# Sample tokens kept in residue order modulo 16 through the attention of an encoder layer

## The chip, the cores and the metric

The kernel runs on one core of one Trainium2 chip. The metric is device microseconds of one execution; lower is better. TensorE is called PE, VectorE DVE, ScalarE ACT, GpSimd POOL and SyncE SP in the rows. PEld is the loading of PE's stationary operand, which overlaps its matmuls.

## The reference

One encoder layer is applied to a prompt of 256 tokens and to a sample sequence of 2048 tokens, width 1024. A mixing sublayer projects the normed input into u, q, k and v; u goes through a state-space branch, q, k and v through attention of 8 heads of 64, and both are normed, joined and projected. A feed-forward sublayer with a short convolution follows. All operands are float32. The attention is what the change is about:

```python
DILATED_PATTERNS = ((128, 1), (512, 4), (2048, 16))

def dilated_attention(q, k, v):
    slopes = jnp.exp2(-8.0 * jnp.arange(1, N_HEADS + 1, dtype=jnp.float32) / N_HEADS)
    outs, lses = [], []
    for window, dil in DILATED_PATTERNS:
        o, lse = dilated_branch(q, k, v, window, dil, slopes)
        outs.append(o)
        lses.append(lse)
    weights = jax.nn.softmax(jnp.stack(lses, axis=0), axis=0)
    return jnp.sum(weights[..., None] * jnp.stack(outs, axis=0), axis=0)
```

In `dilated_branch`, a pattern of dilation d splits the tokens into d subsequences by their residue modulo d. In each of them a query sees the keys at most 64 places away on either side, with a bias that falls linearly with the distance in tokens and with the slope of the head. The three results are mixed per token by the softmax of their log denominators.

## The kernel before

The program is built in Python with all loops unrolled. A scheduler places the instructions in each engine's queue by a simulated timeline of its own; each engine then runs its queue strictly in order, with semaphores between engines. DMAs are issued from SP's queue, the loads of q and k (L939) and a few others from POOL's.

Stages, in order of time. The first norms the tokens and projects u and v, 256 tokens at a time. The second projects q and k while the state-space branch runs; `qk_d` holds q and k transposed, split into a high and a low part, and `v_d` holds v, all in token order. The third is the attention, from about 680 to 1165 us. The fourth projects the attention's half of the mixture, norms again, and the last two are the feed-forward's up and down projections.

The attention runs over four head pairs `hp`, two heads `h` each. `load_values` fetches the values of a head pair in three layouts, `v1`, `v2`, `v3`, one for each dilation 1, 4 and 16, and `vq` for the prompt. `load_head` fetches `qs` (queries, high part above low part), `kh` and `kl` of one head, 2304 tokens each. A head makes its three patterns in order 0, 1, 2 (dilations 1, 4, 16), then the mixing weights of the patterns, then the prompt's attention, then the join.

A pattern has 16 units of 128 queries. A unit of dilation 1 or 4 scores them against 256 keys, one of dilation 16 against its 128. At the ends of a subsequence there are only 192 keys. The operands are taken from `qs`, `kh` and `kl` by slices with a step of 1, 4 or 16 elements (`span`); queries are the stationary operand, keys the moving one. Units are worked in groups of 512 score columns (`group`): two matmuls for each unit (L967 with `kh`, L968 with `kl`), VectorE adds the bias and finds the row's extreme (L973), ScalarE takes the exponential and its sum (L974), PE transposes the probabilities (L153), and `copy2` evicts them (L957 on ScalarE, L958 on VectorE). `pair` multiplies them with the values (L1004), two units at a time in the two halves of PE's columns; for dilation 16 L1125 does this. An end block has 64 keys where others have 128. ScalarE evicts the outputs to `ot`, back into token order (L1128, L1130, L1133).

GpSimd makes the head's bias tables `bt` from constants (L1073 to L1077). The extreme and the sum of each query (`st`) go through DRAM for patterns 0 and 1 (L1143 writes those of pattern 1), since `weights` wants them with 16 consecutive tokens in a partition (`r01`, L1010); pattern 2 has them so already. `weights` writes the mixing weights to `w_d`; `join` loads them broadcast over partitions (`wb`, L1036), and GpSimd multiplies and adds the three outputs (L1041, L1043) and stores them in `ob_d`.

Between groups, `side_work` lets another piece of work run: in the first head pair the gated unit of the state-space branch (`glu`), later the projection of that branch's output (`project_a`, tile names `pat`, `pah`, `ppa`, `pxt`). Those matmuls are 512 columns wide and stand in PE's queue between those of the attention; `pah` is made by ScalarE and GpSimd (L868). What is left of them is done after the last head, before `project_b` works on the joined outputs, prompt tiles first.

## Time and profile before

| | us |
|---|---|
| three runs | 2893.41 median, 2881.18 to 2896.9 |
| the profiled execution, its own time | 2889.24 |
| its span from first to last instruction | 2887.4 |
| PE busy in the span | 2760.7 |
| VectorE busy | 1864.3 |
| ScalarE busy | 1325.5 |
| GpSimd busy | 649.3 |

The mean granted clock of TensorE over the span is 0.974 of full speed. A slice below is a fortieth of the span, 72 us. [...]

### The profile page before, as it was taken

To read this page: it belongs to the slowest core of one execution; us is meant where nothing else is said; L and a number is where in the kernel's file an instruction comes from. 1 tells how busy PE (TensorE), PEld (TensorE's weight loads), DVE (VectorE), ACT (ScalarE), POOL (GpSimd) and SP (SyncE) were. 2 spreads that over 40 slices of the span, in tenths; PEclk is the share of its full clock that TensorE was granted. 3 is DMA by queue.
4 is the path that set the end of the run, shared out by engine and by line. 5 is a ranking of instruction groups with operands and counts; after the bars stand their busy time and mean duration, and the time that the engine had idled before them with its cause. 6 is when DMAs were issued, how large, how long until landed. Compare 5 with 4: busy or idle time off the path is not lost. (4 is left out here: it accounts for less than half of the span.)

```text
span 2887.4 us, 43596 instructions
## 1 busy us (share of the span) xinstructions
PE 2760.7 (96%) x15488; PEld 2458.3 (85%) x15488; DVE 1864.3 (65%) x4274; ACT 1325.5 (46%) x2723; POOL 649.3 (22%) x1120
## 2 busy tenths in 40 slices
PE   7998989999999999889999999999999989999999
PEld 6787767788778888667999999999999978888887
DVE  5766899976645444597989897778877752223221
ACT  3354455545566666344655565556555531112110
POOL 0587533312243442220111121113100000000000
PEclk9999999999899999999999999999999999999999
DMA  7574888777676775747555564444544452224221
GB/s 214 160 245 138 249 232 233 197 189 166 138 188 159 165 179 134 231 157 255 180 172 179 174 199 155 156 154 138 161 154 152 134 186 83 74 86 141 84 86 47
DMA packets 483990, 471.04 MB, mean 163 GB/s; under 512 B 87984, under 2 KB 406076, under 8 KB 480700
## 3 DMA queue, kind: packets, MB, share of 16 engines
q1 hardware_dynamic: 465084, 425.25, 49.3%
q0 software_dynamic: 18688, 43.01, 6.5%
q8 instruction: 122, 2.00, 0.3%
q14 instruction: 96, 0.79, 0.1%
HBM read 308.63 MB, written 159.55 MB: 162 GB/s over the span
## 5 line engine op out<-in xcount | busy, mean ns | idle before, releaser
L156 PE MATMUL pf<-dw,ah 128*128 128x512 f32 x792 | 309.7, 392 | 4.3 <-ACT dw L1182 4.3
L157 PE MATMUL pf<-dw,ah 128*128 128x512 f32 x792 | 309.4, 391 | 2.0 <-DVE dw L1183 2.0
L158 PE MATMUL pf<-dw,ah 128*128 128x512 f32 x792 | 309.1, 391 | 0.0
L1467 DVE TENSOR_TENSOR acc<-pf,acc 128x512 f32<-128x512 f32 x72 | 49.7, 691 | 379.8 <-PE pf L158 379.7
L1453 ACT ACTIVATE ah<-at 128x512 fp32r<-128x512 f32 x72 | 53.1, 784 | 409.0 <-PE pf L158 409.0
L974 ACT ACTIVATE sb<-sb,st 128x256 f32<-128x256 f32 (+2 forms) x384 | 172.5, 452 | 31.6 <-DVE st L973 30.2
L1182 ACT ACTIVATE uw<-su 128x1024 fp32r<-128x1024 f32 x132 | 139.7, 1058 | 100.4 <-PE pu_5p L1366 5.6
L156 PEld LDWEIGHTS pf<-dw,ah 128*128 128x128 f32 x792 | 149.7, 189 | 37.5 <-ACT dw L1182 6.2
L157 PEld LDWEIGHTS pf<-dw,ah 128*128 128x128 f32 x792 | 149.6, 189 | 33.8 <-DVE dw L1183 3.1
L158 PEld LDWEIGHTS pf<-dw,ah 128*128 128x128 f32 x792 | 149.6, 189 | 31.1
L1183 DVE TENSOR_TENSOR uw<-su,uw 128x1024 fp32r<-128x1024 f32 x132 | 160.8, 1219 | 17.8 <-ACT uw L1182 17.5
L1415 ACT ACTIVATE h<-r,convp 128x767 f32<-128x767 f32 (+2 forms) x132 | 135.5, 1028 | 67.0 <-DVE r L1402 64.3
L1410 POOL COPY r<-edge 128x2 f32<-128x2 f32 x88 | 58.2, 662 | 480.3 <-DVE h L1421 471.5
L1418 DVE SCALAR_TENSOR_TENSOR h<-r,convp,h 128x255 f32<-128x255 f32 (+3 forms) x176 | 139.8, 815 | 39.4 <-ACT h L1415 38.9
L1412 POOL COPY edge<-r 128x2 f32<-128x2 f32 x88 | 73.9, 840 | 357.5 <-DVE r L1402 186.0
L967 PE MATMUL s<-kh,qs 128*128 128x256 f32 (+2 forms) x384 | 151.7, 403 | 0.0
L958 DVE COPY pb<-pt 64x128 f32<-64x128 f32 (+2 forms) x150 | 74.2, 505 | 106.6 <-PE pt L153 92.3
L1421 DVE SCALAR_TENSOR_TENSOR h<-r,convp,h 128x768 f32<-128x768 f32 (+2 forms) x176 | 140.6, 813 | 1.4
L968 PE MATMUL s<-kl,qs 128*128 128x256 f32 (+2 forms) x384 | 137.1, 368 | 0.0
L973 DVE CUSTOM_DVE_ANT_0 sb<-s,bt 128x256 f32<-128x256 f32 (+2 forms) x384 | 120.5, 356 | 18.0 <-PE pt L153 13.2
L500 POOL TENSOR_TENSOR q<-ph,phs 128x64 f32<-128x64 f32 (+6 forms) x352 | 119.5, 372 | 2.1
L1004 PE MATMUL po<-pb,v 128*64 128x128 f32 (+1 forms) x1024 | 115.0, 296 | 0.0
(934 smaller groups left out, 7650.7 us busy)
## 6 DMA issues: line engine op xcount, KB each, us to landing
us<-in_w_up_dram SPq DMA_DIRECT2D x88, 512.0 KB
su<-ws_d SPq DMA_DIRECT2D x88, 512.0 KB
at<-act_d SPq DMA_DIRECT2D x36, 704.0 KB
ws_d<-su SPq DMA_DIRECT2D x44, 512.0 KB
qk_d<-qt SPq DMA_DIRECT2D x72, 256.0 KB
wb<-w_d SPq DMA_DIRECT2D x32, 384.0 KB
us<-in_w_up_dram SPq DMA_DIRECT2D x44, 256.0 KB
ds<-in_w_down_dram SPq DMA_DIRECT2D x44, 256.0 KB
```

What stands on the lines that cost most here:

```text
L156: mm = T.matmul(ps, lhi, rhi, start=first, stop=False)
L157: T.matmul(ps, lhi, rlo, start=False, stop=False)
L158: T.matmul(ps, llo, rhi, start=False, stop=last)
L967: T.matmul(ps[:, c:c + n], qs[:, q], khi[:, keys], start=True, stop=False)
L968: T.matmul(ps[:, c:c + n], qs[:, q], klo[:, keys], start=False, stop=True)
L973: V.tensor_tensor_reduce(sb[:, c:c + n], ps[:, c:c + n], bias, 1.0, 3e38, ALU.add, ALU.min, mn)
L974: A.activation(sb[:, c:c + n], sb[:, c:c + n], AF.Exp, bias=mn, scale=-1.0, accum_out=den)
L1182: A.activation(dst[:, 0], src, AF.Copy)
L1183: V.tensor_tensor(dst[:, 1], src, dst[:, 0].bitcast(F32), ALU.subtract)
L1415: A.activation(h[:, a:b], r[:, a:b], AF.Identity, bias=cw[:, 3], scale=cw[:, 1])
L1418: V.scalar_tensor_tensor(h[:, c0:c1], r[:, c0 - 1:c1 - 1], cw[:, 0], h[:, c0:c1], ALU.mult, ALU.add)
L1421: V.scalar_tensor_tensor(h[:, c0:c1], r[:, c0 + 1:c1 + 1], cw[:, 2], h[:, c0:c1], ALU.mult, ALU.add)
```

## The change

Sample tokens are put into residue order modulo 16 when they are read: tile i of 16 holds the 128 tokens with residue i. `qk_d` and `v_d` keep that order, with one prompt tile ahead of the sample and one behind it (`place`, `S0`, `PQ`). The state-space branch gets its tokens back in order through `u_d`. In the attention, the keys of a unit become runs: 128 contiguous for dilation 16, runs of 32 for dilation 4 and runs of 8 for dilation 1. Queries of dilations 4 and 1 are copied once per head into `q1` and `q0` so that each unit's are contiguous; those of dilation 16 are so already. The bias tables are permuted to match, are stored for the first head and halved in place from head to head. Units at the ends have 256 keys too, with the absent ones masked by the table. The patterns run in order dilation 16, 1, 4; the prompt's attention follows the first of them. The join puts the tokens back in order. The diff, cut:

```diff
+    def blocks(n):
+        i = np.arange(P)
+        at = i % (P // n) * n + i // (P // n)
+        k0, k1 = at - 64, at + 64
+        for k, ok in ((k0, k0 >= 0), (k0, k0 < P), (k1, k1 < P), (k1, k1 >= 0)):
+            d = np.abs(at[:, None] - k[None, :]).astype(np.float64)
+            out.append(np.where((d <= 64) & ok[None, :], d, BIG))
...
+        [ident, eye16, blocks(16) / 2, blocks(4) * 2, far * 8, pd.reshape(P, 512) / 2, pm.reshape(P, 512)], axis=1)
+S0, PQ = P, P + NS
...
+    def place(i, t):
+        if i < NPAIR - 1:
+            return S0 + (i + 8 * t) * P
+        return t * PQ
...
             def load_x(i):
-                    nc.sync.dma_start(out=xt, in_=xrows(i * 2 * P + t * P, P))
+                    src = (x_sample[0].rearrange("(p r) d -> r p d", r=16)[i + 8 * t] if i < NPAIR - 1 else
+                           x_prompt[0, t * P:(t + 1) * P])
...
             def project_u(i):
-                    A.activation(ut[:, m2 * 2 + m, ::-1, (i % 2) * 32:(i % 2) * 32 + 32],
-                                 pu[:, m].rearrange("p (n l) -> p l n", l=L), AF.Copy)
-                if i % 2 or i == NPAIR - 1:
-                    for m in range(4):
-                        nc.sync.dma_start(out=u_d[...], in_=ut[:, m, :, 0:n])
+                            A.activation(o.rearrange("p (n h) -> p h n", h=2),
+                                         pu[:, m].rearrange("p (h n) -> p h n", h=2), AF.Copy)
+                for m in range(4):
+                    if i < NPAIR - 1:
+                        nc.sync.dma_start(out=ud[m][:, L - 1 - i, 0:NCS], in_=ut[:, m])
...
-            ga = zb.tile([P, 4, NB], F32, name=f"ga{b}", tag="ga", bufs=3)
+            ga = zb.tile([P, 4, NB], F32, name=f"ga{b}", tag="ga")
-    gws = pg.enter_context(mkpool(name="wstg", bufs=4, side="right"))
+    gws = pg.enter_context(mkpool(name="wstg", bufs=2, side="right"))
...
     def load_values(hp, behind=None):
+        nc.sync.dma_start(out=v3, in_=v_d[S0:PQ, cs].rearrange("(r p) c -> p r c", p=P))
+        later.append(nc.sync.dma_start(out=vq, in_=rows(0, (1, P), (PQ, 2))))
+        for t in range(17):
+            later.append(nc.sync.dma_start(out=v1[:, t], in_=rows(S0 - 4 + 8 * t, (P, 16), (1, 8))))
+        for g in range(4):
+            for t in range(5):
+                later.append(nc.sync.dma_start(out=v2[:, g, t],
+                                               in_=rows(S0 + g * P - 16 + 32 * t, (4 * P, 4), (1, 32))))
...
     def load_head(hp, h, behind=None):
-            t = kp.tile([P, NT], F32R, name=f"{nm_}{nh}", tag=nm_)
+            t = kp.tile([P, NT], F32R, name=f"{nm_}{nh}", tag=nm_, bufs=1 if nm_ == "qs" else 2)
...
+        qs = tl[0][:, S0:PQ]
+        q0, q1 = [kp.tile([P, NS], F32R, name=f"q{pat}{nh}", tag=f"q{pat}", bufs=1) for pat in range(2)]
+        for j in range(4):
+            js = slice(j * 512, (j + 1) * 512)
+            A.activation(q0[:, js].rearrange("d (u r p) -> d u r p", u=4, r=16),
+                         qs.rearrange("d (r c u p) -> d c u r p", r=16, c=4, u=4)[:, j], AF.Copy)
+            G.tensor_copy(q1[:, js].rearrange("d (u a p) -> d u a p", u=4, a=4),
+                          qs.rearrange("d (a g u p) -> d g u a p", a=4, g=4, u=4)[:, j])
...
         def group(nm, khi, klo, units, normal=False):
-                T.matmul(ps[:, c:c + n], qs[:, q], khi[:, keys], start=True, stop=False)
-                T.matmul(ps[:, c:c + n], qs[:, q], klo[:, keys], start=False, stop=True)
+                T.matmul(ps[:, c:c + n], q, places(khi, *keys), start=True, stop=False)
+                T.matmul(ps[:, c:c + n], q, places(klo, *keys), start=False, stop=True)
...
+            for k in range(4):
+                tr(pt[:, k, :], sb[:, k * P:(k + 1) * P])
+            last_copy[0] = copy2(pb_, pt)
...
         def join(hd, ots):
-                o = [t[:, c * 512:(c + 1) * 512] for t in ots]
+                o = [t.rearrange("d (r p) -> d r p", r=16)[:, :, c * 32:(c + 1) * 32] for t in ots]
+                on = wb[:, 0]
                 for pat in range(3):
-                    E.tensor_tensor(o[pat], o[pat], wb[:, pat], ALU.mult)
+                    E.tensor_tensor(o[pat], o[pat], wb[:, pat].rearrange("d (p r) -> d r p", r=16), ALU.mult)
                     if pat:
-                        E.tensor_tensor(o[0], o[0], o[pat], ALU.add)
+                        E.tensor_tensor(on.rearrange("d (p r) -> d r p", r=16) if pat == 2 else o[0],
+                                        o[0], o[pat], ALU.add)
...
-                G.tensor_scalar(bt[:, 0:256], mid, sl, None, ALU.mult)
...
+                pbt = bp.tile([P, 512], F32, name=f"pbt{nh}", tag="pbt")
+                G.tensor_tensor(pbt, atab[:, C_PD:C_PD + 512], atab[:, C_PM:C_PM + 512], ALU.add)
+                def halve(c0, c1):
+                    if nx < HEADS:
+                        G.tensor_scalar(atab[:, c0:c1], atab[:, c0:c1], 0.5, None, ALU.mult)
+                halve(C_PD, C_PD + 512)
...
-                for pat in range(3):
-                    if pat == 1 and nx < HEADS:
+                for at, pat in enumerate((2, 0, 1)):
+                    if at == 1 and nx < HEADS:
                         head_q[nx // 2, nx % 2] = load_head(nx // 2, nx % 2, done)[0]
...
+                                    q = qp_[0][:, u * P:(u + 1) * P]
+                                    keys = S0 + 8 * u - 4, (8, 2), (P, 16), (1, 8)
...
+                                    q = qp_[1][:, (j * 4 + u) * P:(j * 4 + u + 1) * P]
+                                    keys = S0 + j * P + 32 * u - 16, (32, 2), (4 * P, 4), (1, 32)
...
+                                    keys = S0 + ix * P, (1, P)
+                                    q = places(qs, *keys)
...
+                    halve(*((0, 512), (512, 1024), (C_FAR, C_FAR + P))[pat])
+                    if pat == 2:
+                        pb_ = group(f"p{nh}", kh, kl, [...], normal=True)
...
                     elif pat == 1:
                         for j in range(2):
+                            for a in range(4):
+                                nc.sync.dma_start(
+                                    out=st_d[hd][1, j].rearrange("(u p a g) -> a p u g", p=32, a=4, g=4)[a],
+                                    in_=st[a * 32:(a + 1) * 32, j].rearrange("p (u g) -> p u g", g=4))
```

The evictions to `ot` change their order with it: they write runs of 8 (dilation 1), runs of 32 (dilation 4) and contiguous (dilation 16), where they wrote contiguous, with a step of 4, and with a step of 16.

## Rows read from the trace of the kernel before

**Rows 1.** The page's slices: busy tenths of an engine in 40 equal parts.
```profile
PE   7998989999999999889999999999999989999999
DVE  5766899976645444597989897778877752223221
```
**Rows 2.** Busy time by stage: us, engines busy (instructions), clock, DMA share, GB/s.
```profile
core 0: us, PE busy (x) PEld busy (x) DVE busy (x) ACT busy (x) POOL busy (x), PEclk, DMA share, GB/s
...
620.00:680.00 60.00, 52.01 (x358) 49.52 (x357) 41.20 (x80) 26.88 (x53) 18.59 (x16) 0.89 0.87 213
...
800.00:1160.00 360.00, 356.44 (x2612) 294.31 (x2613) 178.54 (x841) 228.40 (x793) 140.84 (x136) 0.97 0.70 163
```
**Rows 3.** Groups by shape, 800 to 1160 us: busy us, mean ns, idle before.
```profile
L967 PE MATMUL s<-kh,qs 128*128 128x256 f32 x132 | 49.9, 391 | 0.0
...
L967 PE MATMUL s<-kh,qs 128*128 128x128 f32 x96 | 39.8, 414 | 0.0
```
**Rows 4.** Weight loads of line L967: ns min/median/max, first and last start.
```profile
L967 PEld LDWEIGHTS s<-kh,qs x384: 186/309/337, 679.3 to 1156.3; 128*128 128x128 f32 x192
```
**Rows 5.** PE in order of time: start, us; dilation 16, 1, 1 and 4.
```profile
904.70 0.39 PE L967 MATMUL s<-kh,qs 128*128 128x128 f32 x1
...
905.78 0.39 PE L968 MATMUL s<-kl,qs 128*128 128x128 f32 x1
...
928.32 0.28 PE L967 MATMUL s<-kh,qs 128*128 128x256 f32 x1
928.44 0.29 PE L968 MATMUL s<-kl,qs 128*128 128x256 f32 x1
...
940.20 0.25 PE L967 MATMUL s<-kh,qs 128*128 128x192 f32 x1
940.29 0.28 PE L968 MATMUL s<-kl,qs 128*128 128x192 f32 x1
...
943.57 0.52 PE L968 MATMUL s<-kl,qs 128*128 128x192 f32 x1
...
945.10 0.41 PE L968 MATMUL s<-kl,qs 128*128 128x192 f32 x1
```
**Rows 6.** PE in order of time: the PV matmuls of two groups.
```profile
902.90 1.01 PE L1004 MATMUL po<-pb,v 64*64 64x128 f32 x8
...
945.44 0.66 PE L1004 MATMUL po<-pb,v 128*64 128x128 f32 x8
```
**Rows 7.** Line L1139, the copy of pattern 0's statistics, once per head.
```profile
L1139 DVE COPY s<-pts x8: 272/279/279, 712.9 to 1128.0; 32x128 f32<-32x128 f32 x8
```
**Rows 8.** Groups by shape on GpSimd, 800 to 1160 us.
```profile
L1041 POOL TENSOR_TENSOR ot<-ot,wb 128x512 f32<-128x512 f32 x37 | 46.3, 1278 | 102.4 <-DMA wb<-w_d 88.3 <-DMA ob_d<-obp 14.1
...
L1076 POOL TENSOR_SCALAR bt<-atab 128x512 f32<-128x512 f32 x6 | 9.0, 1492 | 0.3
L1077 POOL TENSOR_TENSOR bt<-bt,atab 128x512 f32<-128x512 f32 x6 | 7.8, 1292 | 0.4
```
**Rows 9.** Busy time of GpSimd on tile `bt` alone, 800 to 1160 us.
```profile
800.00:1160.00 360.00, 29.85 (x30) 0.97 0.70 163
```
**Rows 10.** Waits of GpSimd and SP, 800 to 1160 us; SP's issues of line L921.
```profile
POOL ot L1041 <- DMA wb<-w_d: 88.3, 11, 16.8
...
SPq L1010 <- DMA st_d<-st: 14.1, 4, 6.5
...
L921 SPq DMA_DIRECT2D v<-v_d x16: 359/586/1556, 683.5 to 1048.1; - x16
```
**Rows 11.** Groups by shape on ScalarE, 800 to 1160 us: two evictions.
```profile
L1133 ACT ACTIVATE ot<-po 128x512 f32<-128x512 f32 x12 | 12.5, 1046 | 0.0
...
L1128 ACT ACTIVATE ot<-po 128x512 f32<-128x512 f32 x12 | 7.2, 597 | 23.7 <-PE po L1004 23.6
```
**Rows 12.** PE in order of time, after the last head.
```profile
1168.94 0.66 PE L1004 MATMUL pop<-pbp,vq 128*64 128x128 f32 x8 [2.80 <-DVE dd L1024]
...
1212.73 0.50 PE L156 MATMUL pw<-ohib,mix 128*128 128x512 f32 x1 [1.64 <-DVE x L879]
```

## What the change should do to the time, predicted before it ran

> **What bounds the kernel now.** I read the page's slices first, to see which engine is full where [rows 1], then one table of stages [rows 2], then the stage that the diff rewrites: its matmuls by shape and in order of time [rows 3 to 6], the other engines there [rows 7 to 11], and the hand-over to the next stage [rows 12]. In the slices PE stands at eight or nine tenths nearly throughout; the reader should see that VectorE, far below it in the attention (slices 10 to 16), comes near it only later. The stages say it in numbers: from 800 to 1160 us, most of heads 2 to 7 of the attention, PE is busy 356.44 of 360 us, VectorE 178.54, ScalarE 228.40, GpSimd 140.84, at a granted clock of 0.97. No other engine and no transfer ends PE's work there, so this stage is as long as what PE is given, and a nanosecond off a matmul comes off the time until another engine is full. One head takes (1128.0 - 712.9) / 7 = 59.3 us, from the first and the last of the eight copies of the dilation-1 statistics [rows 7].
>
> The table by shape [rows 3] shows something to explain. The score matmuls of 128 columns (the dilation-16 pattern) take 414 ns each on L967, those of 256 columns 391: half the columns, no less time. The stationary operand explains it. The weight load of `qs` on L967 lasts 186 ns at the least and 309 in the median [rows 4]; queries taken with a step of 4 or 16 elements are the slow kind. What this costs is seen in the starts [rows 5]. With contiguous queries (the dilation-1 pattern) 256-column matmuls follow each other by 0.12 us (928.32, 928.44), and a 192-column one is followed after 0.09 (940.20, 940.29). In the dilation-16 pattern, 128 columns, the step is (905.78 - 904.70) / 5 = 0.216. In the dilation-4 pattern it is (945.10 - 943.57) / 6 = 0.255 for a mixture of 192 and 256. So both strided patterns run at the pace of their reads, not of their columns.
>
> A second loss: the eight PV matmuls of a pair of units last 0.66 us where both halves have 128 keys, and 1.01 where an edge block with 64 keys is among them [rows 6]. With equal shapes the two halves start together; with unequal ones they take turns.
>
> **The change, part by part.** I take the sum over all eight heads, with all steps at full clock.
>
> (1) Dilation-4 scores: 8 heads x 16 units x 2 = 256 matmuls. Queries come from the permuted copy `q1`, contiguous; keys become runs of 32. From 0.255 to the 0.12 of contiguous operands: 256 x 0.135 = 35 us off PE.
>
> (2) Dilation-16 scores: 256 matmuls of 128 columns, both operands now contiguous. No row shows this shape with fast loads. Bounds are 0.06 (half of the 256-column step) and 0.12 (that step itself, if the load and not the columns sets it). I take 0.09, the 192-column step, which lies nearest: 256 x (0.216 - 0.09) = 32 us off, between 25 and 40.
>
> (3) Every unit is padded to 256 keys, so every PV pair is of equal shape. Edge groups per head: two of eight in the dilation-1 pattern (blocks 0 and 15), all eight in the dilation-4 pattern; 80 in all. 80 x (1.01 - 0.66) = 28 us off. The dilation-1 pattern's two edge units per head get 64 columns more: 32 matmuls x 0.03 = 1 us added.
>
> (4) Dilation-1 scores: queries come from the copy `q0`, keys change from one contiguous run to runs of 8. I cost it at nothing. The nearest rows are contiguous, 0.12, and steps of four elements, 0.255 [rows 5]; between these it would cost 0 to 256 x 0.135 = 35 us. I take the lower end, because a run of 8 is contiguous seven times in eight. [...] No row here shows runs.
>
> (5) GpSimd. Per head it is busy 140.84 / (360 / 59.3) = 23.2 us [rows 2], and its queue stands for the weights of the join a further 88.3 / 6.07 = 14.5 [rows 10]. The change takes out five bias operations (29.85 us over six heads, 5.0 each [rows 9]) and puts in three halvings of 512, one of 128 and the prompt table: 3.25 x 1.49 + 1.29 = 6.1 [rows 8]. Four `q1` copies of 128x512 at 1.49 at most: 6.0. The join keeps ten operations, but eight (six products, the two last sums) now touch `wb` with a step of 16 elements. With p for one of these, the queue needs 23.2 + 14.5 - 5.0 + 6.1 + 6.0 + 8 (p - 1.28) = 44.8 + 8 (p - 1.28) us a head. PE will need 59.3 - (35 + 32 + 28 - 1) / 8 = 47.5. No row has a strided GpSimd operation; ScalarE's copy of the same size takes 0.597 contiguous and 1.046 with a 16-element step [rows 11], a factor of 1.75, which gives p = 2.24. At p = 1.28 GpSimd is just below PE; at 2.24 it needs 52.5, and 8 x 5.0 = 40 us come back. Only one of three operands is strided, so I take p = 1.75, about midway, 48.6: 8 us back. [...]
>
> What stands behind a waiting GpSimd: the halvings wait for VectorE's last read of a table and the next head's VectorE waits for them; `pah` feeds PE's output projection; the next head's three loads stand in the same queue. That is how a late GpSimd would reach PE.
>
> (6) ScalarE: 228.40 / 6.07 = 37.6 us a head. Four `q0` copies of 0.60 to 1.05 add 2.4 to 4.2; the dilation-16 eviction becomes contiguous and the dilation-1 eviction strided, about even. That makes about 41 of 47.5. It still fits, but the `q0` copies wait in its queue for the load of `qs` and for PE's last use of the single `q0` buffer, with exponentials behind them. 0 to 24 us (3 a head); I take 8.
>
> (7) Order 3-1-2. The dilation-4 statistics are now last, so at each head's end they pass through DRAM: eight issues instead of two, at 0.59, then the landing, which `r01`'s load on SP's queue waits for, 14.1 / 4 = 3.5 us a time [rows 10]. Behind it on SP stand the tile stores and loads of the output projection; heads 0 to 6 hide this. After the last head the join gets its weights some 6 x 0.59 + 3.5 = 7 us later, and its strided operations take 4 x 0.47 = 2 more. PE there has leftover projections until 1212.73 and then the two prompt tiles before it needs the join's output [rows 12], and the prompt group moves forward and takes its 2.80 us gap along. Cost 0 to 10; I take 4.
>
> (8) Other loads: values take 39 issues per head pair instead of 17, 4 x 22 x 0.59 = 52 us of SP's queue [rows 10], spread over heads; the packets stay 512 B. `u` goes out in longer runs with 36 issues for 20; x, v and q/k rows keep their sizes. DMA's share, 0.70, becomes 0.70 x 59.3 / 47.5 = 0.87, which 620 to 680 us shows as sustained [rows 2]. The first head's copies and the smaller buffers `ga` and `gws` fall beside the gated unit: 0 to 6 us, I take 3.
>
> Sum: -35 - 32 - 28 + 1 + 8 + 8 + 4 + 3 = -71. The profiled execution took 2889.24 us (span 2887.4), inside the shown runs, 2881 to 2897 with a median of 2893.41. 2889 - 71 = **2818 us**.
>
> **Rivals.** (A) GpSimd or another queue becomes the bound of a head. For it: 44.8 of 47.5 us even without any penalty. Against: part of its waiting can hide other work. At p = 2.24, 32 us more come back than in the sum: 2850, and up to 2870 if DMA near its full share delays the loads too.
>
> (B) Runs read as slowly as steps. Then (4) costs 35 and (1) gains nothing: 2818 + 35 + 35 = 2888, no change; if only the runs of 8 pay, 2853. For it: no row shows runs. Against it: the slow rows have every element apart, and a run has few such places.
>
> (C) Slower: GpSimd's strided operations in the join. The price is p; the head is again as long as before when 44.8 + 8 (p - 1.28) = 59.3, at p = 3.09, 2.4 times the contiguous row. At p = 3.6 a head takes 63.4: 2889 + 8 x 4.1 + 15 for terms (6) to (8) = 2937. ScalarE's factor of 1.75 speaks against.
>
> (D) PE loses its slow loads, but the head's dependence chain (scores, VectorE, exponential, transpose, copy, PV) with ScalarE at 41 / 47.5 leaves it idle, and most of the gain goes: 2875 to 2890.
>
> **How the numbers follow.** Forecast, 2790 to 2848: 0.50. Better still (clean queues, 0.06 in (2)), below 2790: 0.09. A, 2848 to 2872: 0.18. B, 0.08, half of it without change. D, 0.08, mostly without change. C, 0.07. The range leaves out C, most of D and the far half of B, and some of the better end: 2780 to 2868. A difference under 0.5% (14 us) can't be told from none. Faster: 0.50 + 0.09 + 0.18 + 0.04 + 0.02 = 0.83; same 0.10; slower 0.07.
>
> **What would show it.** Steps of 0.12 for all 256-column scores and near 0.09 for 128; L967's weight loads all near 190 ns; no 64-row matmul, PV eights at 0.66; heads some 49 us apart; the join's products at 1.7 us or so; PE still busy over 95% of the stage. PE idle behind `pah`, a halved table or a next head's load means A or C; score steps of 0.2 mean B; idle behind ScalarE's exponentials or `q0`, D. A head of 50 us with the time not lower would mean that the hand-over, or a later stage, gave it back.

## The result and the profile after

The changed kernel takes 2960.69 us in the median (2954.06 to 2964.98), the kernel before 2893.26 beside it. The ratio is 1.0239, 95% interval 1.0203 to 1.0274: slower, where 2818 was forecast. The profiled execution took 2954.06 us (span 2952.3), 65 more than before's.

Two views of after, the slices of the page and the table of stages (PE, PEld, DVE, ACT and POOL busy us with instructions, granted clock, DMA share, GB/s), to be read against [rows 1, 2]. The slices:

```profile
PE   7989889997777787888899999999999989999999
DVE  6666799976645454568898897777877752223221
```

And the stages:

```profile
680.00:800.00 120.00, 88.00 (x804) 79.29 (x805) 79.03 (x281) 65.00 (x219) 38.86 (x35) 0.84 0.65 147
800.00:1160.00 360.00, 274.95 (x2354) 230.93 (x2354) 175.90 (x739) 205.89 (x709) 154.28 (x146) 0.88 0.65 151
```

In the attention PE, full before, is now busy 275 of 360 us, and no other engine has taken its place: all have holes. The granted clock is 0.88 for 0.97. Over the whole span PE's busy time fell from 2760.7 to 2690.2 us, so its work did become cheaper; its idle time grew by 135 us. The marker of a head [rows 7] in after:

```profile
L1188 DVE COPY s<-pts x8: 354/372/374, 725.1 to 1187.6; 32x128 f32<-32x128 f32 x8
```

That is (1187.6 - 725.1) / 7 = 66.1 us a head, for 59.3 before and 47.5 that PE was to need. By the starts of PE's instructions: from the first score to the last PV of a sample token the attention takes 536.5 us (486.7 before), from there to the first matmul of the prompt's output projection 60.4 (46.6). What follows is 5 us longer, and what comes before the attention 4 us shorter.

The matmuls themselves do nearly what was forecast. PE in order of time (start, us): a PV eight, two scores of dilation 4 that follow each other, the first and last of four of dilation 16 and of four of dilation 1.

```profile
945.98 0.66 PE L1031 MATMUL po<-pb,v 128*64 128x128 f32 x8
...
998.97 0.29 PE L1004 MATMUL s<-kh,q 128*128 128x256 f32 x1
999.09 0.29 PE L1005 MATMUL s<-kl,q 128*128 128x256 f32 x1
...
1005.73 0.28 PE L1004 MATMUL s<-kh,qs 128*128 128x128 f32 x1
...
1006.07 0.27 PE L1005 MATMUL s<-kl,qs 128*128 128x128 f32 x1
...
1012.77 0.28 PE L1004 MATMUL s<-kh,q 128*128 128x256 f32 x1
...
1013.15 0.29 PE L1005 MATMUL s<-kl,q 128*128 128x256 f32 x1
```

The weight loads of the contiguous queries `q0` and `q1` on L1004, ns min/median/max:

```profile
L1004 PEld LDWEIGHTS s<-kh,q x256: 186/190/338, 695.9 to 1195.6; 128*128 128x128 f32 x128
```

Groups by shape on GpSimd and ScalarE, 800 to 1160 us (busy us, mean ns, idle before):

```profile
L1069 POOL TENSOR_TENSOR ot<-ot,wb 128x512 f32<-128x512 f32 x33 | 50.7, 1562 | 118.0 <-DMA wb<-w_d 99.4 <-DMA st_d<-st 18.6
...
L1071 POOL TENSOR_TENSOR wb<-ot,ot 128x512 f32<-128x512 f32 x11 | 14.3, 1300 | 0.2
L978 POOL CAST q<-qs 128x512 fp32r<-128x512 f32 x24 | 14.3, 636 | 10.8 <-PE s L1005 10.7
...
L976 ACT ACTIVATE q<-qs 128x512 fp32r<-128x512 f32 x20 | 10.9, 617 | 37.2 <-DMA qs<-qk_d 37.2
```

The steps between starts, shorter than the 0.27 to 0.29 that one of these scores lasts, are 0.11 for 128 columns, 0.12 for 256 with keys in runs of 32, and 0.13 with keys in runs of 8. The weight loads' median is 190 ns for 309 [rows 4]. The strided products of the join cost 1.56 us, and a strided sum 1.30. What is new is waiting. Five of the largest waits from 800 to 1200 us (who <- what: us in total, times, longest):

```profile
POOL ot L1069 <- DMA wb<-w_d: 123.0, 12, 17.9
...
PE s L1004 <- DVE st L1013: 38.9, 6, 13.6
ACT q L976 <- DMA qs<-qk_d: 37.2, 5, 10.0
DVE mm L1043 <- DMA r<-st_d: 36.8, 6, 12.5
...
PE po L1031 <- ACT ot L1163: 25.2, 5, 7.8
```

VectorE's `mm` is the first operation of the mixing weights. It waits for the statistics, and the next head's bias operations, for which PE waits, stand behind it. ScalarE's `q0` copies wait for `qs`, with exponentials and the evictions to `ot` behind them. Each names a late transfer. Why they are late is seen, in one place, in SP's queue in the first head of a pair, head 4 (start, time in the queue, line, count):

```profile
962.67 2.26 SPq L954 DMA_DIRECT2D v<-v_d  x4
965.03 1.16 SPq L1075 DMA_DIRECT2D ob_d<-wb  x2
966.23 1.21 SPq L954 DMA_DIRECT2D v<-v_d  x2
969.37 1.51 SPq L1063 DMA_DIRECT2D wb<-w_d  x2
970.92 30.19 SPq L954 DMA_DIRECT2D v<-v_d  x14
...
1008.11 1.09 SPq L1075 DMA_DIRECT2D ob_d<-wb  x2
1012.28 1.29 SPq L1063 DMA_DIRECT2D wb<-w_d  x2
1013.63 6.28 SPq L1194 DMA_DIRECT2D st_d<-st  x8
1021.23 0.38 SPq L1037 DMA_DIRECT2D r<-st_d  x1
```

PE's next score, in order of time (in brackets its idle time and what ended it):

```profile
1026.54 0.58 PE L1004 MATMUL s<-kh,q 128*128 128x256 f32 x1 [13.10 <-DVE st L1013]
```

Fourteen value loads hold the queue for 30 us. GpSimd had finished the first half of head 3's join at 991; its store goes out at 1008, the second half's weights, which must wait for that store because the sum now lies in `wb`, at 1012, head 4's own dilation-4 statistics behind them, and `r01` at 1021. PE has then stood 13 us.

### The profile page after: what moved, and what is told of

Same layout as the page of the kernel before. It is cut to its first block, busy times and chain, and to the rows that moved or that the text cites. A ratio compares the mean times of both kernels' runs of the same rounds, so it can differ in the third digit from the quotient of the medians.

```text
span 2952.3 us, 43769 instructions
## 1 busy us (share of the span) xinstructions
PE 2690.2 (91%) x15488; PEld 2404.7 (81%) x15488; DVE 1875.6 (64%) x4224; ACT 1326.4 (45%) x2725; POOL 683.9 (23%) x1148
## 5 line engine op out<-in xcount | busy, mean ns | idle before, releaser
L1014 ACT ACTIVATE sb<-sb,st 128x256 f32<-128x256 f32 (+1 forms) x384 | 177.1, 463 | 49.6 <-DVE st L1013 46.5
L174 PE MATMUL pt<-ctab,sb 128*128 128x128 f32 x640 | 106.9, 293 | 26.3 <-ACT sb L1014 25.8
L1031 PE MATMUL po<-pb,v 128*64 128x128 f32 x1024 | 92.3, 319 | 40.8 <-ACT ot L1163 25.2
L1013 DVE CUSTOM_DVE_ANT_1 sb<-s,atab 128x256 f32<-128x256 f32 x216 | 82.8, 416 | 55.4 <-PE pt L174 51.1
L1004 PE MATMUL s<-kh,q 128*128 128x256 f32 x256 | 79.7, 333 | 38.9 <-DVE st L1013 38.9
L174 PEld LDWEIGHTS pt<-ctab,sb 128*128 128x128 f32 x640 | 77.2, 148 | 46.1 <-ACT sb L1014 27.7
```

The source lines that it names most:

```text
L174: T.transpose(out, in_, ident[:n, :n])
L1014: A.activation(sb[:, c:c + n], sb[:, c:c + n], AF.Exp, bias=mn, scale=-1.0, accum_out=den)
L1031: T.matmul(po[half * ST:(half + 1) * ST], segs[half][j], pb_[:, half * n + j, :], start=j == 0, stop=j == n - 1)
```

## The experiments

All of them edit the kernel after, except e4. Ratios are to the kernel before on the same chip; after itself is 1.0239.

| run | edit | us | ratio, 95% interval |
|---|---|---|---|
| e1 | weights later | 3003.1 | 1.0404, 1.0385 to 1.0423 |
| e2 | q0, q1 copies later | 2950.4 | 1.0220, 1.0203 to 1.0237 |
| e3 | both | 2994.0 | 1.0374, 1.0356 to 1.0393 |
| e4 | before, with the new order | 2896.0 | 1.0027, 1.0008 to 1.0047 |
| f1 | e1, two dilation-4 output tiles | 3003.7 | 1.0406, 1.0387 to 1.0425 |
| f3 | f1 and e2 | 2989.0 | 1.0355, 1.0336 to 1.0373 |
| g1 | join's DMAs from GpSimd | 2946.3 | 1.0204, 1.0179 to 1.0229 |
| g3 | f3 and g1 | 2951.9 | 1.0226, 1.0209 to 1.0243 |
| n1 | no value loads after pair 0 | 2909.7 | 1.0079, 1.0056 to 1.0101 |
| h2 | keys loaded later | 2957.6 | 1.0251, 1.0235 to 1.0266 |
| h3 | h2 and e2 | 2956.8 | 1.0242, 1.0220 to 1.0264 |
| h4 | h3 and g1 | 2950.1 | 1.0225, 1.0203 to 1.0248 |
| r1 | few value issues | 2918.7 | 1.0105, 1.0089 to 1.0120 |
| k3 | q/k burst behind the values | 2942.4 | 1.0187, 1.0172 to 1.0203 |
| k5 | k3, e2, head 1's keys later | 2934.0 | 1.0152, 1.0136 to 1.0168 |
| k6 | k5 and g1 | 2953.4 | 1.0219, 1.0197 to 1.0241 |
| r2 | r1 and e2 | 2924.9 | 1.0115, 1.0095 to 1.0135 |
| e5 | contiguous join | 2947.7 | 1.0202, 1.0186 to 1.0217 |

**Is it the waits that the trace names?** e1 moves the weights, e2 the copies, e3 both.

```diff
                             if side_work(hp, ...):          # ahead of it, in the next head:
+                            if owed and at == 1 and g8 == 0 and j == 1:
+                                weights(o_hd, *o_sts, last_bias[0])   # mm behind the last bias
+                                join(o_hd, o_ots)
```

> One edit of the kernel after: VectorE's first operation of a head's mixing weights (and with it the join) stands behind the bias of the next head's second dilation-1 group, some 20 us later in its queue; after the last head nothing is moved. Theory 1 (VectorE's queue stands at each head's end for the dilation-4 statistics, 36.8 us in 800 to 1200, with 38.9 us of PE idle behind it): the wait of mm on r01 nearly vanishes, heads shrink from 66.1 by about 5 us, the time falls by 35 to 60 us to 2900 to 2925. Theory 2 (ScalarE's queue, which stands for qs, is what costs): the time stays above 2945, the idle moves to the other wait. Rival 3 (GpSimd is full): time unchanged, 2950 to 2970.

```diff
-                        head_q[...] = load_head(nx // 2, nx % 2, done)[0]
+                        next_q = load_head(nx // 2, nx % 2, done)[0]
+                    if at == 2 and nx < HEADS:
+                        head_q[...] = order_queries(nx, next_q, done)   # q0, q1 behind the eviction
```

> One edit of the kernel after: the copies q0 (ScalarE) and q1 (GpSimd) of the next head are issued apart from its loads, q0 behind the second dilation-1 eviction of the present head, some 20 us later. Theory 2 (ScalarE's queue stands 37.2 us in 800 to 1200 for qs, with 25.2 us of PE idle behind the evictions): the wait of q0 on qs vanishes and the time falls by 20 to 35 us, to 2925 to 2940. Theory 1 alone: at most 10 us, 2950. Rival 3 (GpSimd full): unchanged.

> Both edits together. If the two queue waits are the whole loss beside the cheaper matmuls, the gains add up: 2960 - 60 to 100 = 2860 to 2900, with heads of about 56 us and the granted clock of 800 to 1160 back above 0.93. If one wait hides the other, clearly more than the sum, down to 2820. If GpSimd's strided join or its waits bind, no better than the better of the two alone (above 2905).

e1 does take VectorE's wait on `r01` away, and is about 1.65% slower still. The waits of e1, 800 to 1200 us:

```profile
PE po L1031 <- ACT ot L1173: 97.1, 5, 22.7
...
ACT ot L1173 <- POOL ot L1073: 75.7, 5, 21.6
```

The first dilation-4 eviction now waits for GpSimd's join of the head before to leave the only buffer of that output. Theory 1 as put falls: the wait marks a late chain, and a delay at one place in it comes back at another. e2's gain is some 0.2% and lies inside the interval; e3 keeps e1's trouble, with PE waiting 103.9 us for that eviction.

**Is it the order?**

```diff
-                for pat in range(3):
+                for at, pat in enumerate((2, 0, 1)):     # in the kernel before; prompt after pat 2
```

> The kernel before with nothing of the change but the order of patterns 3-1-2 and the prompt's group after the dilation-16 pattern; tokens, tables, operands and join as before. Theory 1 (order puts DRAM-bound statistics last, ahead of VectorE's queue): slower than before by 25 to 50 us, 2918 to 2943, with PE idle behind VectorE's mm at each head's end. The prediction's step (7), in which heads 0 to 6 hide it: 2890 to 2900. Fewer DMAs carry the statistics here (2 for 8), so the lower half is likelier than the upper.

0.27% slower, about a tenth of the loss. VectorE's wait in e4, 800 to 1200 us:

```profile
DVE mm L1016 <- DMA r<-st_d: 7.0, 4, 2.9
```

Statistics that pass through DRAM last are not late by themselves (e4 sends them with two issues, after with eight). So "heads 0 to 6 hide this" was right for the order, and something else in the change makes that path long.

**Is it a buffer, or the join's place in SP's queue?** f1 gives the dilation-4 output a second tile, g1 issues the join's loads and stores from GpSimd.

```diff
-                    ot = op.tile([...], tag=f"ot{pat}", bufs=2 if at < 2 else 1)
+                    ot = op.tile([...], tag=f"ot{pat}", bufs=2)     # f1, with e1's edit
```

> As e1_weights_later, but the dilation-4 output tile has two buffers (its 4 KB come from the gated unit's tile ga, one buffer for two). In e1 VectorE's wait on r01 was gone, and PE stood 97.1 us in 800 to 1200 instead for the first dilation-4 eviction, which waited for the join of the head before to leave the only buffer. Theory 1b (late statistics did cost, and e1 only put the join's lateness in their place): that idle vanishes and the kernel is clearly faster than after, 2890 to 2920. Theory 4 (the join itself, with its loads and stores in SP's queue, is the chain that sets a head's length, whatever waits for it): no better than 2945.

> As f1, and the q0 and q1 copies later too (e2's edit, which alone gave 10 us). Theory 1b with theory 2: 2850 to 2890, heads at 52 to 57 us, granted clock above 0.93 in 800 to 1160. Theory 4: above 2930.

```diff
-                    nc.sync.dma_start(out=wb[...                    # g1; ob_d in join likewise
+                    G.dma_start(out=wb[...
```

> One edit of the kernel after: the join's six loads and stores per head (wb, ob_d) are issued from GpSimd's queue instead of SP's, where they stood behind 39 value loads per head pair that wait for their buffers (SP stood so from 984 to 1001 us; the store of a half that GpSimd had done at 991 was issued at 1008, and the next half's wb after it at 1012). Theory 4: GpSimd's 123 us of waiting for wb in 800 to 1200 halves, statistics and weights behind the join's DMAs on SP come sooner, and the time falls by 20 to 50 us, to 2910 to 2940. Theory 1 (statistics through DRAM in VectorE's queue, whatever SP does): less than 15 us off, above 2945. GpSimd's issues cost it 8 x 0.58 us a head; if its queue is full, slower than after.

> f3 and g1 together. If the waits are in series round one loop (statistics, weights, join, buffers), the three together free PE: 2820 to 2860 and PE busy above 0.92 of 800 to 1160, below before's 2885 to 2893. If GpSimd's own work of some 32 us a head with its in-order waits binds, no better than f3.

f1 is no faster than e1 in time, though its heads are. The markers of e1, f1 and g3:

```profile
L1195 DVE COPY s<-pts x8: 353/371/374, 731.3 to 1242.2; 32x128 f32<-32x128 f32 x8
...
L1195 DVE COPY s<-pts x8: 357/371/378, 755.6 to 1240.0; 32x128 f32<-32x128 f32 x8
...
L1202 DVE COPY s<-pts x8: 358/372/383, 751.1 to 1182.7; 32x128 f32<-32x128 f32 x8
```

A head takes (1242.2 - 731.3) / 7 = 73.0 us in e1, 69.2 in f1 and 61.7 in g3, for 64.2 in g1, but the first marker of f1 comes 24 us later than e1's, and that of g3 15 us later than g1's. The second output tile took its 4 KB from the gated unit's `ga`, one buffer for two, and the gated unit runs in the first head pair. That this is the reason is likely and was not shown apart; the times of f1, f3 and g3 therefore don't say what the second tile is worth.

f1 also shows a cause in one place. SP in order of time:

```profile
863.78 0.76 SPq L1037 DMA_DIRECT2D r<-st_d  x1
...
866.67 14.94 SPq L891 DMA_DIRECT2D pat<-at_d  x2
```

GpSimd at the same time:

```profile
864.12 0.54 POOL L967 DMA_DIRECT2D qs<-qk_d  x1 [0.73 <-issue]
...
865.67 1.07 POOL L967 DMA_DIRECT2D kl<-qk_d  x2
```

And VectorE's first operation of the weights:

```profile
887.88 0.18 DVE L1043 TENSOR_TENSOR mm<-r 128x16 f32<-128x16 f32 x1 [19.37 <-DMA r<-st_d]
```

`r01`, 32 KB, is issued at 863.8 and lands at 887.9. Between them run the next head's q and k, 3.5 MB from GpSimd's queue, and two issues of SP stand 15 us. In after such a burst lies at 975 to 993 us. By the packets that start in each 5 us from 975 to 990, SP's transfers move 3 to 11 GB/s in it, GpSimd's 214 to 221. From a burst's first 9 KB packet to its last SP's get 8 GB/s in this one, and 10 to 47 in the attention's other six. Of the value loads' 30 us, 18 fall into it. g1 is some 0.35% faster than after at the middle, but their intervals overlap; the time of g3 is no better, with the late first marker in it.

**The value loads.** n1 leaves them out, r1 makes their issues few, k3 keeps them and moves the burst behind them.

```diff
-            v1, v2, v3, vq = load_values(hp, ld if hp == 0 else None)
+            if hp == 0:
+                v1, v2, v3, vq = load_values(hp, ld)
```

> The kernel after without the value loads of head pairs 1 to 3 (the values of pair 0 are used for all, so the outputs of six heads are not the reference's): 117 of 156 issues of SP's queue and 6 MB less. Theory 5 (SP's queue is what stands: in 963 to 1001 us it issued 20 value loads, one of which stood 11.3 us and two over 4 us while the loads of the next head's q and k held the transfer engines; the join's store, its second wb, the statistics and r01 came behind them): the intervals between heads, which alternate between 55 and 75 us, become even at some 56 to 60, and the time falls by 30 to 60 us, to 2900 to 2930. Theory 1 without it (the path of the statistics by itself): at most 15 us, above 2945.

```diff
-        for t in range(17):
-            later.append(nc.sync.dma_start(out=v1[:, t], in_=rows(S0 - 4 + 8 * t, (P, 16), (1, 8))))
+        later.append(nc.sync.dma_start(out=v1, in_=rows(0, (1, P), (P, 17))))     # v2: 4 for 20
```

> The kernel after with the value tiles v1 and v2 of a head pair filled by 1 and 4 issues of the same bytes and 512-byte packets instead of 17 and 20; the rows they bring are not the right ones, so the outputs are not the reference's. Leaving all value loads of pairs 1 to 3 out gave 51 us (2909.7). If it is the number of issues in SP's queue that costs: 2910 to 2930. If it is the bytes and when they go (they meet the 17 us burst of the next head's q and k, in which one issue of SP stands up to 16 us): at most 15 us off, 2945 to 2960.

```diff
+                    if h == 1 and hp:
+                        wait_for(ld, v_last[0])          # load_head, behind the last value load
```

> One edit of the kernel after: in an even head of pairs 1 to 3 the burst of the next head's q and k waits until the last of the pair's value loads has landed; nothing else moves. Theory 6b (SP's queue stands 62.8 us in value loads in 680 to 1200, 20 us a pair, because they meet the burst): that standing falls below 20 us, the interval from even to odd head shrinks from about 70 towards 60, and the time falls by 20 to 45 us, to 2915 to 2940. If the burst and with it q0 now come too late for the next head, or if it is the issue count alone: within 10 us of after.

n1 takes two thirds of the loss away, r1 nearly as much: 1.0239 - 1.0079 is 1.60% of before, 46 us, and 1.34% is 39. The issues of the dilation-4 values, 680 to 1200 us (ns min/median/max), in after:

```profile
L954 SPq DMA_DIRECT2D v<-v_d x80: 510/796/15985, 691.0 to 1129.5; - x80
```

in r1:

```profile
L952 SPq DMA_DIRECT2D v<-v_d x16: 518/792/4177, 688.8 to 1072.1; - x16
```

and in k3:

```profile
L956 SPq DMA_DIRECT2D v<-v_d x80: 510/796/2752, 693.2 to 1105.7; - x80
```

r1 moves the same bytes in 512-byte packets (its rows have other addresses, though) with a fifth of these issues, and none stands over 4.2 us, for 16.0 in after. In k3 no issue meets the burst and none stands over 2.8, but `qs` comes later for it (ScalarE waits 54.2 us for it in 800 to 1160, 37.2 in after): k3 gets 15 us (0.52%) and leaves 80 issues in the queue. So of the loss that hangs on the value loads, most goes with the edit that makes them few, and a part with their meeting the burst; the two overlap. That r1's other addresses do nothing to the time is assumed. The attention, from the first score to the last PV, in before, in after and in n1:

```profile
679.40:1166.20 486.80, 475.16 (x3517) 395.12 (x3515) 266.31 (x1159) 297.60 (x1012) 169.97 (x165) 0.96 0.69 158
...
675.60:1212.10 536.50, 410.54 (x3563) 348.06 (x3561) 281.76 (x1112) 301.99 (x1017) 208.49 (x192) 0.87 0.63 148
...
680.10:1168.20 488.10, 407.59 (x3563) 346.41 (x3561) 278.79 (x1110) 300.80 (x1016) 207.66 (x192) 0.90 0.60 141
```

n1's attention is as long as before's, and its marker's distance is (1146.5 - 731.9) / 7 = 59.2 us: what before needs, not 47.5. PE is busy 68 us less than before and idle 81 us instead of 12, while no other engine is busy for more than 301 of the 488 us. Three waits make up most of PE's idle time in n1 from 800 to 1160 us:

```profile
PE po L1031 <- DVE pb L995: 17.1, 4, 15.9
...
PE po L1031 <- ACT ot L1164: 15.6, 4, 5.2
...
PE s L1004 <- DVE st L1013: 13.0, 7, 4.6
```

Behind the first of them, ScalarE in order of time:

```profile
799.60 0.72 ACT L189 ACTIVATE ohia<-wsoa,gains 128x512 fp32r<-128x512 f32 x1 [16.80 <-DMA wsoa<-in_w_out_dram]
```

The last two are the waits of after on ScalarE's and VectorE's queues, made shorter. The 15.9 us is another late load: ScalarE stands 16.8 us for `wsoa`, weights of the output projection, while head 2's q and k come in a burst at 780 to 801 us, and VectorE's copy for PE stands behind it. After has it too, 16.0 us of PE's idle time at 783 to 799. What n1 still takes over before, 0.79%, lies mostly behind the attention: from its last PV to the output projection it takes 61.0 us, after 60.4 and before 46.6. In r1 these are 492.0 us for the attention and 63.2 behind it.

**Do the rest of the waits add up?** h2 loads a head's keys one pattern later, to split the burst; h3, h4, k5, k6 and r2 join edits.

```diff
+                    if at == 2 and nx < HEADS:
+                        nk = load_head(nx // 2, nx % 2, done, ("kh", "kl"))[0]
```

> One edit of the kernel after: kh and kl of the next head are issued one pattern later than its qs (at the start of the dilation-4 pattern instead of that of dilation 1), so that 3.5 MB no longer come in one burst of 17 us at 215 GB/s, in which SP's transfers get 3 to 11 GB/s, but in two of about 6 and 11. Theory 6 (the burst is what holds SP's transfers, and with them the statistics): 15 to 40 us off, 2920 to 2945. Theory 5 without the burst (issue count alone): within 10 us of after. If the second burst now meets the statistics at the head's end: slower, to 2980.

> h2 and e2 together: keys one pattern later, q0 and q1 copies later. With both causes apart, gains add: 10 more than h2, 2910 to 2935.

> h3 and g1 together: the join's transfers also leave SP's queue (g1 alone 14 us). If each wait was its own: 2895 to 2920; if they were one wait seen three times, no better than the best of h3 and g1.

> k3 with e2's edit (q0 and q1 copies later, 10 us alone) and, for head 1 alone, the keys one pattern later (in that head the burst met the gated unit's zt loads, which stood 17 us in SP's queue; h3's first interval was 50.4 for 80.0). Gains add if these are separate: 2890 to 2920. If PE then reaches its 47.5 to 50 us a head in most heads: 2850 to 2880, below before.

> k5 with g1's edit (join's transfers from GpSimd's queue, 14 us alone). If SP's queue, once free of the standing, carries the join as well: no better than k5 by 5 us either way. If the join is still late: 10 to 20 us below k5.

> r1 (5 issues of the same bytes for v1 and v2 instead of 37; the rows are not the right ones, so the outputs are not the reference's) with e2's edit (q0 and q1 copies later). In r1 the evictions behind the q0 copies still kept PE idle for 27.8 us in 800 to 1160, five times some 5.6. If the two causes are separate: 2885 to 2905, no slower than before by more than 0.5%, and what is left against the 2818 of the prediction is idle of other kinds. If the freed time is lost to another late transfer, as in e1 and h3: 2910 to 2925.

They don't add. A wait of h3, 800 to 1160 us:

```profile
PE s L1011 <- DMA kh<-qk_d: 51.9, 5, 17.6
```

Two of r2, the same stretch:

```profile
ACT ot L1170 <- POOL ot L1073: 41.7, 5, 16.5
...
PE po L1033 <- ACT ot L1170: 37.1, 5, 23.1
```

In h3 the keys' issue stands in GpSimd's queue behind a join that waits for `wb`, and PE waits for the keys. In r2 the copies no longer hold ScalarE, and the dilation-4 eviction waits for the join instead, as in e1. k5 (1.0152) is the fastest of the versions that leave nothing out and load the right rows, 0.9% below after; k6 gives that back. None of them beats before.

**The join's stride.**

```diff
-                    E.tensor_tensor(o[pat], o[pat], wb[:, pat].rearrange("d (p r) -> d r p", r=16), ALU.mult)
+                    E.tensor_tensor(o[pat], o[pat], wb[:, pat].rearrange("d (r p) -> d r p", r=16), ALU.mult)
```

> One edit of the kernel after: GpSimd's join reads and writes wb contiguously instead of with a step of 16 elements, so tokens and weights are paired wrongly and the outputs are not the reference's. Per product 1278 for 1560 ns, 1.7 us less a head for GpSimd. Rivals A and C (GpSimd's work sets the head's length): 8 x 1.7 = 14 us or more off, 2946 or less. If GpSimd only waits, for wb: within 8 us of after, 2953 to 2968.

Its products, 800 to 1160 us (ns min/median/max):

```profile
L1069 POOL TENSOR_TENSOR ot<-ot,wb x33: 1251/1274/1832, 821.2 to 1148.1; 128x512 f32<-128x512 f32 x33
```

A product takes 1.27 us in the median, for 1.54 in after, and the time is some 0.37% or 11 us lower at the middle, its interval overlapping after's. That is about the work saved, 8 x 6 x 0.27 = 13 us: the join's own time seems to lie on the path, though in after GpSimd is busy for only 154.28 of 360 us and waits for `wb` another 99.4. It would then be a part of a chain, not a full engine; by the interval the gain can also be nothing.

## Why the prediction was wrong

Two steps failed. The first is the premise under the whole sum, that "a nanosecond off a matmul comes off the time until another engine is full". No engine was full, and the nanoseconds did not come off. In after PE's busy time in the attention fell by 65 us and its idle time rose from 12 to 126. With the value loads left out (n1) it is the same at a smaller size, 68 us less busy and 81 idle, and 1.0079 of before's 2889 is still 94 us above the forecast. The second is (8), below, which is worth up to 46.

(1), (2), (3): right for PE's work, with (2) mis-sized. A step of 0.11 and not 0.09 for 128 columns gives 256 x (0.216 - 0.112) = 27 us for 32. In (1) the step is the 0.12 that was forecast, 35 us. PV eights take 0.66 in place of 1.01; in the group of 1.01 [rows 6] the two 64-row matmuls start alone, 0.16 us apart, while in the groups of 0.66 the two halves start within 0.01 us of each other (before at 945.44 us, after at 945.98). Over the span PE's busy time fell by 70 us, at a lower granted clock (in the attention 0.87 for 0.96).

(4): right but for 2 us. Matmuls with runs of 8 follow each other by (1013.15 - 1012.77) / 3 = 0.127 us, contiguous ones by 0.12. Rival B is out.

(5): the price was too high, p = 1.56 for 1.75 for a product, and next to nothing for a strided write (1.30 for 1.29 contiguous [rows 8]). One strided operand of three costs 22% here (1.56 us in after for 1.28 [rows 8]). The `q1` copies cost 0.64 us and not 1.49. Taking the join's stride away (e5) gave between nothing and 22 us, where the term had 8. Rival C, with p above 3.09, is out: the kernel is slower, but not by that mechanism.

(6): named rightly, ScalarE's queue behind `qs`, at 8 us. The trace puts 25 us of PE's idle time there. Taking it away alone (e2) gave about 5, between nothing and 17; that the chain behind was late anyhow is the likeliest reason, and only argued.

(7): half right. The order alone costs 0.27%, 8 us (e4). But behind the last head, where the term had 4 us and at most 10, the time to the output projection grew by 14 us (60.4 for 46.6; e4, with the order alone, has 50.6). And the list of queues was short: the text names SP's queue, and where PE stood 38.9 us is VectorE's, in which `mm` is ahead of the next head's bias. It also missed that the sum of the join now lies in `wb`, so that the second half's load waits for a store, and that the single output tile, still that of the last pattern, now belongs to one of eight groups, which is first evicted earlier in the head.

(8): the term that failed. "39 issues per head pair instead of 17 ... 52 us of SP's queue, spread over heads" was put at nothing: the 3 us of that paragraph are for the first head's copies and the smaller buffers. It is worth 39 us (r1), and 46 with the bytes (n1). The price of an issue was not the main error (0.80 us in the median for 0.59). The issues aren't spread: the dilation-4 values become free only at the end of the odd head, so 20 issues come at once, they meet the burst of q and k, one stands up to 16 us, and everything that the head's end needs (statistics, `r01`, weights, `wb`, the join's stores) stands behind them in order. The prediction treated SP as an engine with 6.5 us a head more to do. It is the one queue through which a chain runs six times a head (statistics out, `r01`, weights out, `wb`, the join's store, `wb` again).

Rival A, "GpSimd or another queue becomes the bound of a head", was the nearest, with SP in GpSimd's place, but its 2850 to 2870 supposed a queue that is merely full. It wasn't full. Rival D, a chain that leaves PE idle so that the gain goes, describes n1's attention, but its chain was that of the scores, and the waits of n1 lead mostly to late loads. The account that fits the runs is this: the chain from the statistics to the freed output tile passes SP, VectorE, GpSimd and ScalarE with single buffers (`wb`, `qs`, the dilation-4 tile), and a delay on it can become a delay of the next head. That is how a head could become longer than before (66.1 for 59.3 us) with less work on PE. The waits name each link; that they make one loop is argued, and no run took the whole loop away.

What stays open: with the value loads' issues out of the way 1.05% remains over before, and the 47.5 us a head of the forecast was seen in no version, so it isn't known whether the chain of a head could run at that pace with every load in time. e1, r2 and h3 show where the waits go (output tile, join, keys), but a version with two buffers of `wb`, `qs` and the dilation-4 tile that takes no room from `ga` was not tried, nor was the number of the statistics' issues (eight for two, 6.3 us in SP's queue). The 14 us between the attention and the output projection were not taken apart. Of PE's 88 busy us of 120 at 680 to 800, for 112 before, the wait behind `wsoa` explains 16; no run tested it.

## What to carry to other kernels

Before an edit is costed by what the full engine saves, follow each chain that passes an in-order queue more than once per stage, and ask what else will stand in that queue at that moment; count a transfer's issues at the time when their buffers come free, not on average. A wait that the trace names after a change is where the lateness shows; move it alone and it may come back larger elsewhere, as in e1, so look for the lateness (n1, r1) before mending the wait. And when a run takes room for its edit from somewhere else, read the heads' distance and the time apart, as f1 and g3 needed.

## What the runs showed of the hardware

- While 3.5 MB in packets of 9 KB went through GpSimd's queue at 214 to 221 GB/s, SP's transfers, mostly in packets of 512 bytes, got 3 to 11 GB/s (after, 975 to 990 us); over whole bursts they got 8 in this one and 10 to 47 in the attention's other six. In such bursts a 32 KB load took 24 us to land (f1), and single issues of SP stood up to 16 us (after, L954 at 852.8 us); the median issue of the same line takes 0.80. What sets the two shares was not shown, and the forecast's sum has no term for such a meeting.
- A weight load of contiguous queries takes 190 ns in the median (after, L1004), where the median of before, two of three patterns with a step of 4 or 16 elements, was 309 [rows 4]. 128-column matmuls then follow each other by 0.11 us (after, 1005.73 to 1006.07), hardly less than 256-column ones (0.12, after at 998.97).
- GpSimd copies 128x512 with a cast in 0.64 us (after, L978), and multiplies the same size by a constant in 1.49 [rows 8].
